# Copies for a triangular inverse issued from ScalarE, the last block's first weights split earlier, and merge steps spaced half a unit apart

## The chip, the cores and the metric

The kernel runs on one core of a Trainium2 chip. A core has five engines with a queue of instructions each: TensorE (PE, matrix products into PSUM), VectorE (DVE), ScalarE (ACT), GpSimd (POOL) and SyncE (SP, which here only issues DMAs). Every engine works its own queue in order; an instruction that waits for another engine holds up everything behind it on its engine. DMAs are issued by an instruction in an engine's queue, and the transfer then runs beside the engines.

The metric is the device time of one execution in microseconds. Before the change three runs took 789.44, 790.56 and 791.85 us; the median, 790.56 us, is the time that the change is measured against.

## What is computed

One decoder layer on a sequence of 256 positions and 2048 channels, in float32. One input projection feeds two token mixers, a gated delta rule (A) and a block attention (B); both are widened, gated, merged, projected and added to the input:

```
h = rms_norm(x, pre_norm_w)
proj = h @ w_in                        # q, k, v, z, b, a of A; q, k, v, z of B; gate_a, gate_b
oa = gated_delta_rule(...)             # chunks of 64; per head and chunk a triangular solve:
#   L = tril(kb @ k.T * decay, -1);  T = inverse(L + I);  u = T @ vb;  w = T @ (kb * exp(g))
u_a = (rms(oa) * silu(z_a)) @ w_branch_a
u_b = (attention(...) * silu(z_b)) @ w_branch_b
merged = sigmoid(gate_a) * u_a + sigmoid(gate_b) * u_b
x = x + rms_norm(merged @ w_out, post_norm_w)
```

## The kernel before

**Products in two parts.** Every float32 weight block is loaded into a raw tile of 1 MB (`raw_...`, a pool with three buffers), and split into a high part that ScalarE makes by a cast (`hi`, L218) and a low part, the difference, that VectorE makes (`lo`, L219). Each pool of split tiles has three buffers. TensorE multiplies high and low parts separately. A raw tile is split in two steps of 128x1024 elements; such a step feeds 16 matmuls in a column block of 256 (`proj_t`), 12 in `proj_n` and in a product for two banks, and 6 in a product for one bank. The loads of weights are issued by SyncE, and each waits there until a raw buffer is free, that is, until the low part of an earlier load (or another reader of it) is done.

**Blocks and background work.** The list `ORDER` (L42) gives the order of the projection blocks: q, k, v, gates and so on. Beside the blocks run generators in queues (`Queue`, L47): after every few matmuls a block calls `tick()`, which counts half a unit of each queue's wait down and, when it has run out, takes the generator's next step. A step emits its instructions at this place of the program; `yield w` asks for `w` units of other work first. So the numbers after `yield` decide where background work stands between the matmuls.

**What keeps order.** An instruction wrapped in `pin()` stays, among the pinned ones of its engine, in the order of the program. All matmuls are pinned. The others (casts and subtractions of `split`, copies from PSUM) are put into the queue of their engine by the framework's scheduler, which works with its own estimate of when inputs are ready; so a change of one instruction can move others.

**The triangles.** For branch A each head writes its triangles to DRAM (`l_d`, from GpSimd, L512). `inverse()` then copies all of them back into `lc`, four times, to 32 partitions each (L635, `LC_WAIT` units apart, pinned on SyncE), and inverts them by 63 pairs of VectorE instructions, `tw<-lc,tv` (L643) and `tv<-tv,tw` (L650). The first of these reads all four copies. At this time TensorE works on the first three blocks of A's values (v0, v1 and v2 in the order; their tiles are named v0, v2 and v4, after the first of a block's two heads), 64 matmuls each: 32 pairs of a `hi` and a `lo` matmul, in four steps of eight pairs. After such a block its results go through `halves` (a ScalarE copy L454, a VectorE addition L455) and `conv_silu` (L461 on VectorE, L462 on ScalarE, three times L464 on VectorE, L468 on ScalarE), for two tiles.

**Seven products.** `seven()` multiplies a 2x2 block matrix by seven products p1 to p7 in place of eight, with sums and differences of the operands; it is used for u_a twice (ua0, ua2, each with four quarters of the gate block ga3 or gb2 as `fill` between the products) and for the first half of the output projection. `fourth()` (L784) forms the operand of p4 in place from the raw weights of p2 (`raw21`) and the third difference, in two halves.

**Merge.** `branch(c)` multiplies branch B's output; `weighted()` (L1062) then multiplies the result by its gate (`gb`, L1065) and adds it to A's part (`ga`, L1068). `merge(c)` (L1112) transposes the sum on TensorE (`mt`) and splits it into `mT` (L1123, L1124), for c = 0 and 1 with the sums that the seven products need (L1126 to L1137). It starts a fixed number of units after `branch(c)` is queued.

**The last block.** The output projection has four column blocks. After the seven products come the second halves of blocks 0 and 1 (four products of 24 matmuls, 5.4 us each); then block 3, whose four loads (quarters of its weights, eight steps) are all split first (six of the steps into tiles named `keep_...`, pinned, L1220 and L1221) so that it can run for the first half of the positions and then for the second. `weigh()` squares and weights each finished bank (L1176, L1177), `finish()` normalizes, adds x and stores.

Of the kernel before, what the change touches and what calls it, by code (L numbers as in the profile page):

```python
# [8 lines left out]
F32 = mybir.dt.float32  # L9
# [3 lines left out]
ALU = mybir.AluOpType  # L13
AX = mybir.AxisListType

P = 128
# [8 lines left out]
D_WAIT = 7  # L25
SC_WAIT = 4
L_WAIT = 5
LC_WAIT = (1.5, 1.5, 1.5, 3.5)
INV = (0.6, 2)
SLOW = 8  # L30
T_WAIT = (5, 7, 7)
# [43 lines left out]
def hybrid_layer(  # L75
# [45 lines left out]
    def acc_tile(name):  # L121
        return acc.tile([P, 512], F32, tag="acc", name=name)
# [493 lines left out]
    def inverse():  # L616
        lc = big.tile([P, 64, 64], F32, tag="u1", name="lc")
        tv = big.tile([P, 16, 64], F32, tag="tv", name="tv")
        tw = big.tile([P, 16, 64], F32, tag="tw", name="tw")

        nc.gpsimd.memset(tv, 1.0)
        for g in range(4):
            nc.gpsimd.affine_select(
                out=tv[32 * g : 32 * g + 32],
                in_=tv[32 * g : 32 * g + 32],
                compare_op=ALU.is_equal,
                fill=0.0,
                base=g,
                pattern=[[4, 16], [-1, 64]],
                channel_multiplier=0,  # L630
            )
        yield 1
        for g in range(4):
            pin(
                nc.sync.dma_start(  # L635
                    lc[32 * g : 32 * g + 32].rearrange("p j i -> p (j i)"), l_d.rearrange("b h j i -> (b h) (j i)")
                )
            )
            yield LC_WAIT[g]
        for j in range(63):  # L640
            n, r = j // 4 + 1, 63 - j
            pin(
                nc.vector.tensor_tensor(  # L643
                    tw[:, :n, :r],
                    lc[:, j : j + 1, j + 1 :].to_broadcast([P, n, r]),
                    tv[:, :n, j : j + 1].to_broadcast([P, n, r]),
                    op=ALU.mult,
                )
            )
            pin(nc.vector.tensor_tensor(tv[:, :n, j + 1 :], tv[:, :n, j + 1 :], tw[:, :n, :r], op=ALU.subtract))  # L650
            yield INV[after[0] > 0]
        for g in range(4):
            nc.gpsimd.dma_start(
                t_d.rearrange("b h (c g) i -> g (b h) c i", g=4)[g], tv[32 * g : 32 * g + 32]
            )
        inv.append(big.tile([P, NT, H, 64], F32, tag="tt", name="tt"))
        for p_ in range(2):
            for t in range(NT):
                nc.gpsimd.dma_start(
                    inv[0][p_ * 64 : p_ * 64 + 64, t, :, :], t_d[2 * t + p_].rearrange("h c i -> c h i")  # L660
                )
        yield L_WAIT
# [30 lines left out]
    def ga(c, t):  # L693
        return ga_[:, c, t, :]
# [48 lines left out]
    def product(a, raw, banks, first, name):  # L743

        for u in range(2):
            hi, lo = split(raw[:, 2 * u : 2 * u + 2, :], [P, 2, 512], f"{name}_{u}")
            for kk in range(2):
                k = 2 * u + kk
                for (ah, al), pt, new in zip(a, banks, first):
                    mm(pt, ah[:, k], hi[:, kk, :], start=(new and k == 0), stop=False, skip_group_check=True)  # L750
                    mm(pt, ah[:, k], lo[:, kk, :], start=False, stop=False, skip_group_check=True)
                    mm(pt, al[:, k], hi[:, kk, :], start=False, stop=(k == 3), skip_group_check=True)
                tick()
# [15 lines left out]
    def seven(quarter, s_, tq, w, c, banks, name, fill=lambda i: None, done=lambda b: None):  # L769
        c11, c12, c21, c22 = banks  # L770
        s5 = tq[0][:, 0]
        product([quarter(0, 0)], load(w, 0, c, name), [c21], [True], f"{name}p1")
        fill(0)
        product([s_[0]], tq[0], [c12], [True], f"{name}p5")
        nc.scalar.copy(c11, c21)
        product([s_[1]], tq[1], [c21], [False], f"{name}p6")
        fill(1)
        nc.scalar.copy(s5, c12)
        raw21 = load(w, 1, c, name)
        nc.vector.tensor_tensor(c12, c21, s5, op=ALU.add)  # L780
        product([quarter(0, 1)], raw21, [c11], [False], f"{name}p2")
        product([s_[2]], tq[2], [c21], [False], f"{name}p7")

        def fourth(u):  # L784
            us = slice(2 * u, 2 * u + 2)
            nc.vector.tensor_tensor(tq[1][:, us], raw21[:, us], tq[1][:, us], op=ALU.subtract)

        fourth(0)
        fill(2)
        nc.vector.tensor_tensor(c22, c21, s5, op=ALU.add)  # L790
        fourth(1)
        done(c11)
        product([s_[3]], load(w, 1, c + 1, name), [c12], [False], f"{name}p3")
        fill(3)
        done(c12)
        done(c22)
        product([quarter(1, 1)], tq[1], [c21], [False], f"{name}p4")
        dq.add(later(lambda: done(c21)))
# [249 lines left out]
    def attention(p):  # L1048
# [7 lines left out]
        for m in range(2):  # L1056
            aq[m].add(attend(h + m, qTs[m], kTs[m]))

    def branch(c):
        pb = proj_n(wb, c * 512, ob_tile(), H, f"ub{c}")  # L1060

        def weighted():  # L1062
            yield 1
            for t in range(NT):
                nc.vector.tensor_tensor(gb_tile()[:, c, t, :], gb_tile()[:, c, t, :], pb[t], op=ALU.mult)  # L1065
            yield 0.5
            for t in range(NT):
                nc.vector.tensor_tensor(ga(c, t), ga(c, t), gb_tile()[:, c, t, :], op=ALU.add)  # L1068

        dq.add(weighted())  # L1070

# [37 lines left out]
    sf = big.tile([P, 4, 4, P], F32, tag="u1", name="sums_f")  # L1109
    summed = []  # L1110

    def merge(c, wait=1):  # L1112
        yield wait
        p3s = []
        for t in range(NT):
            pt = aux_tile(f"mt_{c}_{t}")
            for q in range(4):
                tr(pt[:, q * P : (q + 1) * P], ga(c, t)[:, q * P : (q + 1) * P], ident)
            p3 = pt.rearrange("p (k n) -> p k n", n=P)
            p3s.append(p3)  # L1120
            hi = mT[:, 4 * c : 4 * c + 4, t * P : (t + 1) * P]
            lo = mT[:, 4 * c : 4 * c + 4, S + t * P : S + (t + 1) * P]
            nc.scalar.copy(hi, p3)  # L1123
            nc.vector.tensor_tensor(lo, p3, hi.bitcast(F32), op=ALU.subtract)  # L1124
            if c == 0:
                nc.scalar.copy(sf[:, t], p3)  # L1126
            yield 0.5
        if c == 1:
            nc.vector.tensor_tensor(sf[:, 2], p3s[1], sf[:, 1], op=ALU.add)
            nc.vector.tensor_tensor(sf[:, 3], sf[:, 2], sf[:, 0], op=ALU.subtract)  # L1130
            yield 0.5
            nc.vector.tensor_tensor(sf[:, 1], sf[:, 0], sf[:, 1], op=ALU.subtract)
            nc.vector.tensor_tensor(sf[:, 0], p3s[0], sf[:, 3], op=ALU.subtract)
            for i, j in enumerate((2, 3, 1, 0)):
                yield 1
                nc.scalar.copy(SH[i], sf[:, j])
                nc.vector.tensor_tensor(SL[i], sf[:, j], SH[i].bitcast(F32), op=ALU.subtract)  # L1137
            summed.append(True)
# [7 lines left out]

    for c in range(D // 512):
        branch(c)
        mq.add(merge(c, 2 if c < 3 else 3.5))
        if c == 2:  # L1150
            third(0)

# [44 lines left out]
            (nc.sync if i % 2 == 0 else nc.scalar).dma_start(of[t * P : (t + 1) * P, cs], yw[t][:, cs])  # L1197

    mq.drain()
    for c, banks in ((0, (c11, c21)), (1, (c12, c22))):  # L1200
        for h in range(2, 4):
            product([quarter(0, h), quarter(1, h)], load(wo, h, c, "y"), banks, [False, False], f"y{c}_{h}")
        for t in range(NT):
            weigh(c, t, banks[t])

    c = 3
    pts = [acc_tile(f"a_y{c}_{t}") for t in range(NT)]
    keep = []
    for tg, n in (("g0", 4), ("ga", 4), ("u1", 4)):
        tl = big.tile([P, n, 2, 512], F32R, tag=tg, name=f"keep_{tg}")  # L1210
        keep += [tl[:, i] for i in range(n)]
    parts = []
    for kb in range(KT // 4):
        raw = wraw.tile([P, 4, 512], F32, tag="raw", name=f"raw_y{c}_{kb}")
        nc.sync.dma_start(raw, wo[kb * 512 : (kb + 1) * 512, c * 512 : (c + 1) * 512].rearrange("(k p) c -> p k c", p=P))
        for u in range(2):
            i = kb * 2 + u
            if i < 6:
                hi, lo = keep[2 * i], keep[2 * i + 1]
                pin(nc.scalar.copy(hi, raw[:, 2 * u : 2 * u + 2, :]))  # L1220
                pin(nc.vector.tensor_tensor(lo, raw[:, 2 * u : 2 * u + 2, :], hi.bitcast(F32), op=ALU.subtract))  # L1221
            else:
                hi, lo = split(raw[:, 2 * u : 2 * u + 2, :], [P, 2, 512], f"y{c}_{kb}_{u}")
            parts.append((hi, lo))
            if i in (1, 3):
                weigh(2, i // 2, pts2[i // 2])
    rbs = [so_far(t) for t in range(NT)]
    for t in range(NT):
        for k in range(KT):
# [36 lines left out]
```

## Time and profile before

The profiled execution took 790.14 us, of which 788.4 us are the span from the first to the last instruction; 1.7 us lie around it.

| what | value |
|---|---|
| median of three runs | 790.56 us |
| profiled execution, its span | 790.14 us, 788.4 us |
| VectorE busy, ScalarE busy | 72%, 54% of the span |
| mean DMA rate over the span | 195 GB/s |
| mean granted TensorE clock | 0.993 of full speed |

A row of the timeline or of the chain gives the start in microseconds from the span's start, then the duration, the engine (PEld is TensorE's weight load), the line, the operation, what is written and read, and, in brackets, how long the engine stood idle before it and what ended that. A row of the waits gives who waited for whom: microseconds in total, number of times, and the longest.

### The profile page before, as it was taken

The page shows a single profiled execution, that of the slowest core. Times are in us where ns is not written, and L with a number is a line of the kernel's source. Part 1 is how long each engine was busy: PE and PEld are TensorE (multiplying, and loading weights), DVE is VectorE, ACT ScalarE, POOL GpSimd, SP SyncE. Part 2 cuts the span into 40 slices and gives each one's busy share as a digit, 9 for nine tenths or more (in the row PEclk, how much of TensorE's full clock was granted, in tenths as well). Part 3 has the DMA queues.
Part 4 walks back from the last instruction along what each step waited for, and adds up shares of the span by engine and source line. Part 5 has one row for each costly group of instructions (what it writes and reads, how often), then busy time and mean ns, then how long its engine had stood idle before and what let it go on. Part 6 is the DMA issues. An engine that isn't in the chain of part 4 may idle for free.

```text
span 788.4 us, 10352 instructions
## 1 busy us (share of the span) xinstructions
PE 767.6 (97%) x3923; PEld 652.3 (83%) x3923; DVE 566.0 (72%) x914; ACT 425.1 (54%) x642; POOL 31.5 (4%) x57
## 2 busy tenths in 40 slices
PE   8999999999799999999999999999999999999986
PEld 7898988898588888888888888788887888877864
DVE  5777679886676899775546786775758677877663
ACT  5676665657344444454447574654455544555551
POOL 3000001111000000002001000000000000000000
PEclk9999999999899999999999999999999999999998
DMA  8485666468655657658434557566656855476632
GB/s 307 161 244 202 198 196 170 133 186 220 211 177 197 194 179 204 174 160 241 129 108 165 210 166 257 196 225 225 195 179 214 309 175 200 170 267 215 212 107 107
DMA packets 93656, 153.44 MB, mean 195 GB/s; under 512 B 3237, under 2 KB 46886, under 8 KB 92966
## 3 DMA queue, kind: packets, MB, share of 16 engines
q1 hardware_dynamic: 89094, 136.51, 54.6%
q0 software_dynamic: 3936, 15.21, 5.5%
q10 hardware_dynamic: 576, 1.05, 0.4%
q8 instruction: 31, 0.51, 0.3%
q14 instruction: 19, 0.16, 0.1%
HBM read 149.61 MB, written 3.15 MB: 194 GB/s over the span
## 4 chain that ended last, share of the span: by engine, by line
PE 92%; DVE 4%; ACT 3%; issue 1%; DMA 1%; SPq 0%; DVEq 0%; ACTq 0%
PE a_gb L144 11%; PE a_ga L144 11%; PE a_y L144 10%; PE a_zg L144 6%; PE a_mk L144 6%; PE a_k L144 6%; PE a_v L144 6%; PE a_zm L144 6%; PE a_ub L144 5%; PE a_mq L144 5%; PE a_mv L144 5%; PE a_q L144 4%; PE a_ua L144 4%; PE sv L144 2%; PE s L144 1%
## 5 line engine op out<-in xcount | busy, mean ns | idle before, releaser
L144 PE MATMUL a_ga<-hi_ga,hT 128*128 128x512 f32 x256 | 82.2, 393 | 0.0
L144 PE MATMUL a_gb<-hi_gb,hT 128*128 128x512 f32 x256 | 79.9, 390 | 0.0
L219 DVE TENSOR_TENSOR lo_gb<-raw_gb,hi_gb 128x1024 fp32r<-128x1024 f32 x32 | 38.7, 1223 | 26.1 <-ACT hi_gb L218 26.0
L144 PEld LDWEIGHTS a_gb<-hi_gb,hT 128*128 128x128 f32 x256 | 48.1, 188 | 10.0
L144 PEld LDWEIGHTS a_ga<-hi_ga,hT 128*128 128x128 f32 x256 | 48.1, 188 | 9.8
L219 DVE TENSOR_TENSOR lo_ga<-raw_ga,hi_ga 128x1024 fp32r<-128x1024 f32 x32 | 38.8, 1222 | 19.0 <-ACT hi_ga L218 18.9
L144 PE MATMUL a_v<-hT,hi_v 128*128 128x512 f32 x128 | 47.2, 411 | 5.0 <-ACT hi_v L218 5.0
L144 PE MATMUL a_gb<-lo_gb,hT 128*128 128x512 f32 x128 | 50.4, 394 | 0.5 <-DVE lo_gb L219 0.4
L218 ACT CAST hi_ga<-raw_ga 128x1024 fp32r<-128x1024 f32 x32 | 33.6, 1053 | 31.7 <-PE a_ga L144 18.4
L144 PE MATMUL a_ga<-lo_ga,hT 128*128 128x512 f32 x128 | 50.1, 391 | 0.4 <-DVE lo_ga L219 0.4
L218 ACT CAST hi_gb<-raw_gb 128x1024 fp32r<-128x1024 f32 x32 | 33.4, 1052 | 31.6 <-PE a_gb L144 28.1
L144 PE MATMUL a_zg<-hi_zg,hT 128*128 128x348 f32 (+1 forms) x192 | 47.0, 322 | 0.0
L144 PE MATMUL a_mq<-hT,hi_mq 128*128 128x512 f32 x128 | 46.7, 405 | 0.0
L144 PE MATMUL a_mk<-hT,hi_mk 128*128 128x512 f32 x128 | 46.1, 402 | 0.0
L144 PE MATMUL a_q<-hT,hi_q 128*128 128x512 f32 x128 | 45.7, 397 | 0.0
L144 PE MATMUL a_y<-hi_y,mT 128*128 128x512 f32 x144 | 45.5, 389 | 0.0
L144 PE MATMUL a_ub<-hi_ub,obT 128*128 128x512 f32 x128 | 41.0, 393 | 0.0
L144 PE MATMUL a_zm<-hi_zm,hT 128*128 128x512 f32 x128 | 40.6, 392 | 0.0
L144 PE MATMUL a_k<-hT,hi_k 128*128 128x512 f32 x128 | 40.5, 399 | 0.0
L144 PE MATMUL a_mv<-hi_mv,hT 128*128 128x512 f32 x128 | 40.1, 391 | 0.0
L144 PE MATMUL a_v<-hT,lo_v 128*128 128x256 f32 x128 | 36.9, 288 | 0.5 <-DVE lo_v L219 0.5
L144 PE MATMUL a_q<-hT,lo_q 128*128 128x256 f32 x128 | 35.9, 280 | 0.0
(375 smaller groups left out, 1965.9 us busy)
## 6 DMA issues: line engine op xcount, KB each, us to landing
raw_ga<-in_w_in_dram SPq DMA_DIRECT2D x16, 1024.0 KB, 5.2
raw_gb<-in_w_in_dram SPq DMA_DIRECT2D x16, 1024.0 KB, 5.2
raw_y<-in_w_out_dram SPq DMA_DIRECT2D x15, 1024.0 KB, 5.1
raw_q<-in_w_in_dram SPq DMA_DIRECT2D x8, 1024.0 KB, 5.7
raw_mv<-in_w_in_dram SPq DMA_DIRECT2D x8, 1024.0 KB, 5.1
raw_v<-in_w_in_dram SPq DMA_DIRECT2D x8, 1024.0 KB, 10.7
raw_zm<-in_w_in_dram SPq DMA_DIRECT2D x8, 1024.0 KB, 5.1
raw_mq<-in_w_in_dram SPq DMA_DIRECT2D x8, 1024.0 KB, 5.9
```

The costliest lines, as they stand in the source:

```text
L144: return pin(nc.tensor.matmul(*args, **kwargs))
L218: nc.scalar.copy(hi, raw)
L219: nc.vector.tensor_tensor(lo, raw, hi.bitcast(F32), op=ALU.subtract)
```

## The change

Five edits, the first four of them to where instructions stand, the last to the order of loads and splits at the end:

1. The four copies into `lc` are issued from ScalarE instead of SyncE, with other distances (1.5, 1.5, 1.5, 3.5 units become 2, 2, 2, 2.5, and the first `yield 1` becomes 0.5; the sum stays 9 units).
2. `fourth()` is pinned, so that its two VectorE instructions stand where the program has them: after the splits of p7, and after the split of the third fill.
3. `weighted()` does its four instructions one by one, half a unit apart.
4. `merge(c)` starts when `weighted()` of that c is done, not after a fixed wait.
5. The first two quarters of block 3's weights are loaded and split between the products of blocks 0 and 1 (`last_parts`), and the banks are weighed in another order.

```diff
-LC_WAIT = (1.5, 1.5, 1.5, 3.5)
+LC_WAIT = (2, 2, 2, 2.5)
...
-        yield 1
+        yield 0.5
         for g in range(4):
             pin(
-                nc.sync.dma_start(
+                nc.scalar.dma_start(
                     lc[32 * g : 32 * g + 32].rearrange("p j i -> p (j i)"), l_d.rearrange("b h j i -> (b h) (j i)")
                 )
             )
...
         def fourth(u):
             us = slice(2 * u, 2 * u + 2)
-            nc.vector.tensor_tensor(tq[1][:, us], raw21[:, us], tq[1][:, us], op=ALU.subtract)
+            pin(nc.vector.tensor_tensor(tq[1][:, us], raw21[:, us], tq[1][:, us], op=ALU.subtract))
...
+    merged = []
...
             for t in range(NT):
                 nc.vector.tensor_tensor(gb_tile()[:, c, t, :], gb_tile()[:, c, t, :], pb[t], op=ALU.mult)
-            yield 0.5
+                yield 0.5
             for t in range(NT):
                 nc.vector.tensor_tensor(ga(c, t), ga(c, t), gb_tile()[:, c, t, :], op=ALU.add)
+                yield 0.5
+            merged.append(c)
...
-    def merge(c, wait=1):
-        yield wait
+    def merge(c):
+        while c not in merged:
+            yield 0.5
...
-        mq.add(merge(c, 2 if c < 3 else 3.5))
+        mq.add(merge(c))
...
+    def last_parts(kb):
+        raw = load(wo, kb, 3, "y")
         for u in range(2):
             i = kb * 2 + u
             if i < 6:
...
+    for c, banks in ((0, (c11, c21)), (1, (c12, c22))):
+        for h in range(2, 4):
+            product([quarter(0, h), quarter(1, h)], load(wo, h, c, "y"), banks, [False, False], f"y{c}_{h}")
+            if h == 2:
+                last_parts(c)
+        for t in range(NT):
+            weigh(2 * c, t, (pts2 if c else banks)[t])
+    c = 3
+    pts = [acc_tile(f"a_y{c}_{t}") for t in range(NT)]
+    for kb in range(2, 4):
+        last_parts(kb)
+    for t in range(NT):
+        weigh(1, t, (c12, c22)[t])
```

More of the change, by code (lines that the diff above doesn't have):

```diff
@@ L1199, in hybrid_layer @@
     mq.drain()
[L1200 to L1207, printed above, removed]
     keep = []
@@ L1212, in hybrid_layer @@
     parts = []
-    for kb in range(KT // 4):
-        raw = wraw.tile([P, 4, 512], F32, tag="raw", name=f"raw_y{c}_{kb}")
-        nc.sync.dma_start(raw, wo[kb * 512 : (kb + 1) * 512, c * 512 : (c + 1) * 512].rearrange("(k p) c -> p k c", p=P))
+    def last_parts(kb):
+        raw = load(wo, kb, 3, "y")
         for u in range(2):
@@ L1222, in hybrid_layer @@
             else:
-                hi, lo = split(raw[:, 2 * u : 2 * u + 2, :], [P, 2, 512], f"y{c}_{kb}_{u}")
+                hi, lo = split(raw[:, 2 * u : 2 * u + 2, :], [P, 2, 512], f"y3_{kb}_{u}")
             parts.append((hi, lo))
-            if i in (1, 3):
-                weigh(2, i // 2, pts2[i // 2])
+    for c, banks in ((0, (c11, c21)), (1, (c12, c22))):
[11 more added lines that the diff above has]
+        weigh(1, t, (c12, c22)[t])
     rbs = [so_far(t) for t in range(NT)]
```

## The prediction

> **What bounds the kernel now.** I read the page first: the head line, the busy times, the shares of the chain of waits.
>
> ```profile
> span 788.4 us, 10352 instructions
> PE 767.6 (97%) x3923; PEld 652.3 (83%) x3923; DVE 566.0 (72%) x914; ACT 425.1 (54%) x642; POOL 31.5 (4%) x57
> PE 92%; DVE 4%; ACT 3%; issue 1%; DMA 1%; SPq 0%; DVEq 0%; ACTq 0%
> ```
>
> TensorE is busy 97% of the span and holds 92% of the chain. The change touches no matmul, so it can only remove or add stalls of TensorE (or half clock after one). Next, the waits of PE:
>
> ```profile
> PE a_v L144 <- ACT hi_v L218: 5.0, 1, 5.0
> PE a_y L144 <- ACT keep_g L1220: 1.8, 1, 1.8
> PE a_y L144 <- DVE lo_y L219: 1.2, 2, 0.7
> PE a_y L144 <- DVE keep_g L1221: 0.8, 1, 0.8
> PE a_ga L144 <- DVE lo_ga L219: 0.4, 1, 0.4
> PE a_gb L144 <- DVE lo_gb L219: 0.4, 1, 0.4
> ```
>
> Each edit stands beside one of these: 1 at a_v, 2 at a_ga and a_gb, 2 to 4 at lo_y, 5 at keep_g. Third, I read the timeline around each.
>
> **Edit 1, the values.** Timeline and windows (columns: us, then PE, PEld, DVE, ACT, POOL busy, granted clock, DMA share, GB/s) at the start of the third block, and the chain's row for the matmuls before:
>
> ```profile
> 181.11 19.79 PE a_v L144 x112
> 203.42 0.28 PE L144 MATMUL a_v<-hT,lo_v 128*128 128x256 f32 x1
> 203.74 0.37 ACT L454 COPY y_v<-a_v 128x256 f32<-128x256 f32 x1 [0.98 <-PE a_v L144]
> 204.24 0.42 DVE L455 TENSOR_TENSOR y_v<-a_v,y_v 128x256 f32<-128x256 f32 x1
> 204.69 0.42 DVE L461 TENSOR_TENSOR xp<-y_v,rrow 128x256 f32<-128x256 f32 x1
> 205.69 1.53 DVE L464 SCALAR_TENSOR_TENSOR y_v<-xp,pcol,y_v 128x256 f32<-128x256 f32 x3 [0.58 <-ACT y_v L462]
> 207.25 0.42 ACT L468 ACTIVATE y_v<-y_v 128x256 f32<-128x256 f32 x1 [1.59 <-DVE y_v L464]
> 207.57 2.92 ACT L218 CAST hi_v<-raw_v 128x1024 fp32r<-128x1024 f32 x3
> 208.63 2.36 DVE L219 TENSOR_TENSOR lo_v<-raw_v,hi_v 128x1024 fp32r<-128x1024 f32 x2 [1.02 <-ACT hi_v L218]
> 208.65 0.79 PE L144 MATMUL a_v<-hT,hi_v 128*128 128x512 f32 x1 [4.95 <-ACT hi_v L218]
> 209.91 0.58 PE L144 MATMUL a_v<-hT,lo_v 128*128 128x256 f32 x1 [0.47 <-DVE lo_v L219]
> 214.07 0.40 PE L144 MATMUL a_v<-hT,hi_v 128*128 128x512 f32 x1
> 192.40:203.70 11.30, 11.30 (x65) 9.52 (x63) 7.60 (x15) 4.81 (x9) 0.00 (x0) 1.00 1.01 267
> 203.70:207.10 3.40, 0.00 (x1) 0.00 (x0) 2.68 (x7) 1.30 (x3) 0.00 (x0) 1.00 0.77 281
> 207.10:214.00 6.90, 4.88 (x14) 3.80 (x15) 4.33 (x8) 3.24 (x4) 0.00 (x0) 0.51 0.25 71
> ```
>
> A pair of matmuls takes 19.79/56 = 0.353 us, a block of 32 pairs 11.3; so the blocks end at 192.4 and 203.7. The third should have started at about 203.54 and reached its eighth pair (14 matmuls on, by the x14 of the last window) at 203.54 + 7 x 0.353 = 206.01; it did so at 214.07. Price of the present stall: **8.06 us**, of which 5.11 is the late start (208.65 - 203.54) and 2.95 the lo wait and the half clock (0.51 from 207.1). Cause: on ScalarE the third block's first cast stands behind the whole copy and convolution of the second block. That order is the scheduler's, not the copies'.
>
> In the built program of the change the order on ScalarE is another:
>
> ```
> hi_v0_1_0, hi_v0_1_1, copy 1 into lc, table load, Silu zg x2, copies 2 and 3 into lc,
> y_v0 (L454), y_v1 (L454), hi_v2_0_0, hi_v2_0_1, L462 x2, copy 4 into lc, Silu y_v0, Silu y_v1,
> hi_v2_1_0, hi_v2_1_1, hi_v4_0_0, hi_v4_0_1, y_v2 (L454) ...
> ```
>
> The third block's casts (hi_v4) now stand ahead of the second's convolution: the old stall goes, all 8.06. But the second block's first cast (hi_v2_0_0) stands behind the copy of the first block's second tile, which waits for that block's last matmul. So a stall arises at 192.4, where the window from 192.40 shows none. With the durations above: copy 192.44 to 192.81; cast to 193.86 (2.92 for three, 1.05 as one started alone); first hi matmul at 193.9, 1.4 late. On VectorE the order is L455, L461 twice, then lo: 192.94 + 0.45 + 0.45 = 194.2 after the L455 of 0.42, and lo takes 1.22 (2.36 for two) to 195.4; the second matmul starts at 195.48 where 192.47 + 0.12 was due: 2.9. Then six L464 of 0.51 (1.53 for three) and two Silu of 0.42 stand before hi_v2_1_0: lo 194.2 to 195.4, two steps of lo and six L464 until 199.6, Silu to 200.0, cast to 201.05, lo to 202.3, against a due time of 195.4 + 16.5 x 0.353 = 201.2: 1.1 more. New stalls 2.9 + 1.1 = 4.0; **net -4.1** (8.06 at best; nothing if the new wait grows to the price of the old). I take the value by these rows, since each duration is measured 11 us later on the same instructions.
>
> The clock: in the trace TensorE stood still from 203.70, and the half clock shows from 207.1, 3.4 us on. The new idle pieces are 1.4 and 1.5 us with a matmul between, so I keep full clock. [...]
>
> The four issues move onto ScalarE. Issue cost and landing:
>
> ```profile
> L635 SPq DMA_DIRECT2D lc<-l_d x4: 338/424/462, 184.1 to 185.5; - x4
> DMA to landing us min/median/max: 7.1/10.1/13.2
> DMA to landing us min/median/max: 5.6/10.7/15.7
> L1197 ACTq DMA_DIRECT2D out_dram<-yw x4: 338/338/374, 773.8 to 784.9; - x4
> ```
>
> (second row: tile lc; third: raw_v). An issue from ScalarE takes 0.34 us; copies 1 to 3 fall where the order above has it waiting for TensorE anyway, the fourth where VectorE is the later: 0 (at most 4 x 0.34 = 1.4). On SyncE the weight loads pass the copies; they wait there for raw buffers, not for the copies: 0. Copy 4 is issued only at about 195.9, and VectorE has the first tw, which needs it, ahead of every lo of the third block, due with the 4.0 above at 203.7 + 4.0 - 1.4 = 206.3. So it may take 10.4 us to land. It lands beside one load, not beside three copies and a load: I take the least of its row, 7.1, so 203.0. Cost 0; at 15.7 it would be 5.3 late.
>
> [...]
>
> **Edit 2, u_a.** The pinned subtraction (L786, 1.22) before the second fill:
>
> ```profile
> 505.68 1.22 DVE L786 TENSOR_TENSOR tq_z<-raw_ua,tq_z 128x1024 f32<-128x1024 f32 x1
> 506.82 2.35 DVE L219 TENSOR_TENSOR lo_ga<-raw_ga,hi_ga 128x1024 fp32r<-128x1024 f32 x2
> 507.33 0.39 PE L144 MATMUL a_ga<-hi_ga,hT 128*128 128x512 f32 x1
> 508.09 0.50 PE L144 MATMUL a_ga<-lo_ga,hT 128*128 128x512 f32 x1 [0.37 <-DVE lo_ga L219]
> 514.75 2.58 DVE L219 TENSOR_TENSOR lo_ua0p<-tq_g,hi_ua0p 128x1024 fp32r<-128x1024 f32 x2 [1.49 <-ACT hi_ua0p L218]
> DMA to landing us min/median/max: 5.0/5.2/6.6
> ```
>
> The lo matmul is at 508.09 instead of 507.33 + 0.23 (a step in these stretches): -0.53, twice (a_ga, a_gb). Pinned, the same 1.22 stand in front of the third fill's lo after 517.3: about +0.4 of stall there, and the next gate load, which by the built order waits for the buffer that the third fill's lo frees, issues at 517.33 + 0.6 + 2.35 = 520.3 instead of 517.3 (0.6 is the addition between); by the last row (tile raw_gb, 5.2 median) it lands at 525.5, just late: +0.4; with 6.6 it is 1.4 more. Net +0.25 each: **+0.5** (-1.1 if the cover holds; +0.5 + 2 x 1.4 = +3.3).
>
> **Edits 2 to 4, merge and y.**
>
> ```profile
> 676.47 0.69 DVE L1132 TENSOR_TENSOR sums_f<-sums_f 128x512 f32<-128x512 f32 x1
> 698.12 0.39 PE L144 MATMUL a_y<-hi_y,mT 128*128 128x512 f32 x1
> 699.24 0.50 PE L144 MATMUL a_y<-lo_y,mT 128*128 128x512 f32 x1 [0.73 <-DVE lo_y L219]
> ```
>
> Here lo waits behind the gate additions (the wait row: 1.2 over two places). Spaced out, and with merge tied to them, both go: -1.2. In return the built order puts 11 such additions (0.69, 0.6 from start to start) between two splits of branch B: 11 x 0.6 + 1.2 = 7.8 us, where the splits of a product of 24 matmuls have 24 x 0.23 = 5.5 and their buffers hold a step or two more; I take 0.5 of the 2.3 as late, an estimate (0 to 1.6). And L786 stands before one more lo of y, as at u_a: +0.4. **Net -0.3** (-1.2 to +1.0).
>
> **Edit 5, the last block.**
>
> ```profile
> 755.06 0.39 PE L144 MATMUL a_y<-hi_y,mT 128*128 128x512 f32 x1
> 757.22 0.50 PE L144 MATMUL a_y<-keep_g,mT 128*128 128x512 f32 x1 [1.77 <-ACT keep_g L1220]
> 758.48 2.81 PE L144 MATMUL a_y<-keep_g,mT 128*128 128x512 f32 x11 [0.76 <-DVE keep_g L1221]
> ```
>
> With half of the weights split before, TensorE goes on at its step of 0.23: (757.22 - 755.06 - 0.23) + (758.48 - 757.22 - 0.23) = 1.93 + 1.03 = **-2.96**. The moved splits (casts of 1.0, subtractions of 1.2) lie beside products of 5.4 us that have two splits each; with two more VectorE has 4 x 1.2 = 4.8. Without that cover the gain would be 0.
>
> **Sum** against the profiled 790.14: -4.1 + 0.5 - 0.3 - 3.0 = -6.9, so 783.2; the profiled run lies 0.42 under the median 790.56, so **783.6** on the median.
>
> **The rivals.**
> - *The new wait also halves the clock.* For: the old one did. Against: pieces of 1.5 us. It would add the 2.95 of the old wait, less the 1.1 that the second stall then absorbs: +1.9, 785.5.
> - *The wait only moves.* One of the largest waits goes from the third block to the second at its whole price, since a copy still waits for a block's end; copies 2 and 3 are built together, so "in turn" isn't what runs. Edit 1 gains nothing: 783.6 + 4.1 = 787.7. For: the order above. Against: only the copy, not the convolution, precedes the cast.
> - *All gains are eaten:* edit 1 at 0, edit 5 half, and u_a at its bound: 783.6 + 4.1 + 1.5 + 2.8 = 792.0 at worst, about 790.5 with half of that load's lateness.
> - *Slower: copy 4 lands late.* The first tw holds VectorE's queue, every lo of the third block behind it, and TensorE waits. It decides from 10.4 us of landing; at 13.2 it costs 2.8, at 15.7 5.3 and, being over 3.4 us of idleness, the 2.95 of half clock: 791.9; at 17 us 793.2. For: the row of raw_v has 15.7 behind four copies. Against: one load beside it.
>
> **How the numbers follow.** Forecast 780 to 785: 0.55; clock 0.12; wait moves 0.17; gains eaten 0.08; slower 0.08. What can be told from no change is 0.3%, 2.4 us. Of the moved wait 0.11 counts as faster and 0.06, where u_a's bound adds to it, as the same; gains eaten as the same. Faster 0.55 + 0.12 + 0.11 = 0.78, same 0.14, slower 0.08. The range goes from 780.0 (edit 1 with half of its new stalls, 783.6 - 2.0, and u_a without its cost, -1.6) to 789.5, which leaves out late copies and eaten gains; the forecast's own is 780 to 785.
>
> **What would show it.** Right: no wait of keep_g; a_y without the 1.2; the third block at full clock; at 192.4 a wait of a_v for hi_v of 1.4 and for lo_v of 1.5 with the clock at 1.00, another of about 1 at 201. Wrong: a clock near 0.5 after 195; the first tw ending after 206 with lo_v behind it; a wait of a_ga for the raw tile's DMA over 1 us; a new wait in block 0 or 1 of y.

## The result and the profile after

The changed kernel took 782.22 us, the median of four executions (782.20 to 782.77), against 790.59 (four executions): a ratio of 0.9896, 95% interval 0.9878 to 0.9913. A second set of four on another chip gave 783.64 (782.76 to 784.46) against 790.48, 0.9911 (0.9895 to 0.9927). So the change saves 6.8 to 8.4 us; the prediction was 783.6.

Page and waits of the changed kernel, as shown of before:

```profile
span 780.4 us, 10345 instructions
PE 765.1 (98%) x3923; PEld 651.2 (83%) x3923; DVE 564.1 (72%) x914; ACT 424.7 (54%) x642; POOL 31.5 (4%) x57
...
PE a_v L144 <- DVE lo_v L219: 1.4, 2, 0.8
PE a_v L144 <- ACT hi_v L218: 1.4, 1, 1.4
PE a_ga L144 <- DVE lo_ga L219: 0.7, 2, 0.4
PE a_gb L144 <- DVE lo_gb L219: 0.4, 1, 0.4
PE a_y L144 <- DVE lo_y L219: 0.4, 1, 0.4
```

The 5.0 of a_v for hi_v has become 1.4, in another place; both waits for keep_g are gone; lo_y has one wait in place of two, lo_ga two in place of one.

Since the 3923 matmuls are the same, each can be compared with its twin. TensorE's place against before (negative: earlier), read from the starts of the same matmul in both traces, gives a ledger of the span:

```
place in the program                  after - before   step of it     forecast
first block of values begins              +0.10           +0.10          0
values done                               -4.25           -4.35         -4.1
before ua0                                -4.35           -0.10          0
after ua0                                 -3.88           +0.47         +0.25
after ua2                                 -3.57           +0.31         +0.25
branch B done                             -3.11           +0.46   }
seven products of y, blocks 0 and 1       -4.39           -1.28   }     -0.3
block 3 done                              -8.03           -3.64         -3.0
```

The last row is the whole difference of the spans, 788.43 - 780.40. The +0.46 at branch B is not a wait: four transposes of a merge stand behind the last matmul of branch B before (it starts at 694.71) and ahead of it in the changed kernel (691.60). The first row is of before, the second of the changed kernel:

```profile
694.94 0.60 PE L147 MATMUL mt<-ident,ga 128*128 128x128 f32 x4
690.00 0.60 PE L147 MATMUL mt<-ident,ga 128*128 128x128 f32 x4
```

So TensorE does this work earlier, and the next row gets the 0.46 back: without it, branch B is at 0 and y at -0.82.

**Values.** TensorE, ScalarE and VectorE from the start of the second block to that of the third, then two windows of 3.41 us with the granted clock:

```profile
192.54 0.37 ACT L454 COPY y_v<-a_v 128x256 f32<-128x256 f32 x1 [2.46 <-PE a_v L144]
192.81 1.99 ACT L218 CAST hi_v<-raw_v 128x1024 fp32r<-128x1024 f32 x2
193.91 0.51 PE L144 MATMUL a_v<-hT,hi_v 128*128 128x512 f32 x1 [1.41 <-ACT hi_v L218]
193.95 1.22 DVE L219 TENSOR_TENSOR lo_v<-raw_v,hi_v 128x1024 fp32r<-128x1024 f32 x1
194.08 0.31 ACTq L635 DMA_DIRECT2D lc<-l_d  x1
195.23 0.38 PE L144 MATMUL a_v<-hT,lo_v 128*128 128x256 f32 x1 [0.81 <-DVE lo_v L219]
201.67 0.39 PE L144 MATMUL a_v<-hT,lo_v 128*128 128x256 f32 x1 [0.63 <-DVE lo_v L219]
202.19 1.05 ACT L218 CAST hi_v<-raw_v 128x1024 fp32r<-128x1024 f32 x1 [0.88 <-DMA raw_v<-in_w_in_dram]
202.67 0.22 DVE L643 TENSOR_TENSOR tw<-lc,tv 128x63 f32<-128x63 f32 x1
203.27 1.23 DVE L219 TENSOR_TENSOR lo_v<-raw_v,hi_v 128x1024 fp32r<-128x1024 f32 x1 [0.38 <-ACT hi_v L218]
205.40 0.36 ACT L454 COPY y_v<-a_v 128x256 f32<-128x256 f32 x1
207.19 0.40 PE L144 MATMUL a_v<-hT,hi_v 128*128 128x512 f32 x1
207.43 0.28 PE L144 MATMUL a_v<-hT,lo_v 128*128 128x256 f32 x1
...
190.19:193.60 3.41, 2.31 (x14) 1.75 (x12) 1.01 (x3) 1.06 (x2) 0.00 (x0) 1.00 1.02 218
193.60:197.01 3.41, 2.29 (x11) 1.80 (x12) 3.34 (x6) 2.01 (x4) 0.00 (x0) 1.00 0.89 217
```

The three new waits stand where they were forecast. The rows list 1.41, 0.81 and 0.63 us of idle time; by the starts of the twin matmuls they make TensorE 1.57, 1.19 and 0.89 us later, against 1.4, 1.5 and 1.1 forecast. The second is shorter because lo began at 193.95, not 194.2: the two L461 took 0.75 together, not 0.9. Behind the third, TensorE is 3.56 us late in all (forecast 4.0). The clock stayed at 1.00. The third block's first cast, at 202.19, now stands ahead of the copy of the second block's results, at 205.40, and the block starts at 207.19 without a wait. Copy 4 landed 7.97 us after its issue, at 202.05, in time for the first tw at 202.67, whose row shows no idle time. That is 0.62 us for VectorE. For TensorE the margin is larger: the matmul at 207.43 reads the lo of 203.27, which takes 1.23, so by these rows copy 4 could have come some 3 us later (an estimate).

**u_a.** PE, ScalarE and SyncE at the third and the last fill of ua0:

```profile
503.21 0.39 PE L144 MATMUL a_ga<-lo_ga,hT 128*128 128x512 f32 x1
512.22 1.22 DVE L786 TENSOR_TENSOR tq_z<-raw_ua,tq_z 128x1024 f32<-128x1024 f32 x1
514.62 0.50 PE L144 MATMUL a_ga<-lo_ga,hT 128*128 128x512 f32 x1 [0.37 <-DVE lo_ga L219]
515.73 0.37 SPq L766 DMA_DIRECT2D raw_ga<-in_w_in_dram  x1
521.04 2.00 ACT L218 CAST hi_ga<-raw_ga 128x1024 fp32r<-128x1024 f32 x2 [2.52 <-DMA raw_ga<-in_w_in_dram]
523.40 0.50 PE L144 MATMUL a_ga<-lo_ga,hT 128*128 128x512 f32 x1 [0.31 <-DVE lo_ga L219]
```

The matmul at 503.21 has lost its wait. The one at 514.62 has it instead, behind the pinned subtraction. And the last gate load, issued at 515.73 (forecast 520.3 - 4.4), lands 5.3 us later; the cast waits for it and the matmul at 523.40 is late, as the prediction has it.

**The end.** The row that stood at 755.06 and the start of block 3:

```profile
750.66 0.39 PE L144 MATMUL a_y<-hi_y,mT 128*128 128x512 f32 x1
750.89 2.43 PE L144 MATMUL a_y<-keep_g,mT 128*128 128x512 f32 x10
```

From 750.66 to 750.89 it is 0.23, the usual step: no wait.

### The profile page after: what moved, and what is told of

The parts are those of the page before. It is cut to its first block, busy times and chain, and to the rows that moved or that the text cites. A ratio compares the mean times of both kernels' runs of the same rounds, so it can differ in the third digit from the quotient of the medians.

```text
span 780.4 us, 10345 instructions
## 1 busy us (share of the span) xinstructions
PE 765.1 (98%) x3923; PEld 651.2 (83%) x3923; DVE 564.1 (72%) x914; ACT 424.7 (54%) x642; POOL 31.5 (4%) x57
## 4 chain that ended last, share of the span: by engine, by line
PE 91%; DVE 3%; ACT 3%; DMA 2%; issue 1%; SPq 0%; DVEq 0%; ACTq 0%
PE a_gb L144 11%; PE a_ga L144 11%; PE a_y L144 10%; PE a_zg L144 6%; PE a_mk L144 6%; PE a_k L144 6%; PE a_ub L144 6%; PE a_zm L144 6%; PE a_mq L144 5%; PE a_mv L144 5%; PE a_v L144 5%; PE a_q L144 4%; PE a_ua L144 3%; PE sv L144 2%; PE s L144 1%
## 5 line engine op out<-in xcount | busy, mean ns | idle before, releaser
L144 PE MATMUL a_v<-hT,hi_v 128*128 128x512 f32 x128 | 45.4, 398 | 1.4 <-ACT hi_v L218 1.4
## 6 DMA issues: line engine op xcount, KB each, us to landing
raw_v<-in_w_in_dram SPq DMA_DIRECT2D x8, 1024.0 KB, 10.7
```

Of the source, the lines that this page charges most:

```text
L144: return pin(nc.tensor.matmul(*args, **kwargs))
```

## The experiments

Each ran beside the kernel before on the same chip; a ratio is against those runs. "Place" is TensorE's place against before, as in the ledger.

**e1_alone: edit 1 alone on the kernel before.**

```diff
-LC_WAIT = (1.5, 1.5, 1.5, 3.5)
+LC_WAIT = (2, 2, 2, 2.5)
...
-        yield 1
+        yield 0.5
...
-                nc.sync.dma_start(
+                nc.scalar.dma_start(
```

> The kernel before with edit 1 alone (the four copies issued from ScalarE, with the new distances). In the built program the order of ScalarE around the value blocks is that of the changed kernel, and the rest is that of before. If the gain of edit 1 is the order of the casts: TensorE is 4.3 us earlier after the value blocks than before, and stays so, the clock stays at 1.00 there, and the span is 788.4 - 4.3 = 784.1 (time about 786.2). If the gain needs the other edits, or most of it came from them: under 2 us.

Ten executions from 785.04 to 789.08, median 787.92, ratio 0.9966 (0.9952 to 0.9980). In the profile the place goes from +1.23 to -2.41: 3.64 gained at the values. The waits there are those of the changed kernel (1.41 and 0.81). But the record of the clock shows a half-speed stretch of 3.41 us from 196.3 (granted 0.53 from 196.08 to 199.49, 0.97 in the next 3.41), and one after the wait for keep_g from 756.1, which costs another 1.03 there. The mechanism holds; the size is cut by a clock that the changed kernel's own profile did not show, and the spread of 4 us is unusual. That became a question of its own (changed_again).

**e1_undone: the changed kernel with the copies back on SyncE.**

```diff
-                nc.scalar.dma_start(
+                nc.sync.dma_start(
```

> The changed kernel with the four copies issued from SyncE again, with the new distances kept. Built, the third block's casts stand behind the second block's convolution again, as before. If the order is what counts: the 4.95 us wait of a_v for hi_v and the half clock come back, and the span is 780.4 + 4.3 = 784.7 (time about 786.6). If it is the distances (copies further apart, less crowding of the weight load): the wait stays away and the time stays at 782.

787.35, ratio 0.9961 (0.9946 to 0.9976). The old wait is back:

```profile
PE a_v L144 <- ACT hi_v L218: 4.9, 1, 4.9
```

and with it 6.83 us at half clock from 208.4. The place goes from +0.57 to +0.91 over the values: nothing gained. So the distances alone do nothing; with them, the move to ScalarE's queue is what flips the scheduler's order. The move with the old distances was not run.

**order_alone, order_on_sync, order_on_scalar: the order written out.** The splits of the second and third block are pinned, the copies of a block's results stand behind the next block's second cast and the convolution behind the fourth:

```diff
-                hi, lo = split(raw[:, :, m * P : (m + 1) * P], [P, 8, P], f"{name}_{kb}_{m}")
+                if held is None:
+                    hi, lo = split(raw[:, :, m * P : (m + 1) * P], [P, 8, P], f"{name}_{kb}_{m}")
+                else:
...
+                    pin(nc.scalar.copy(hi, raw[:, :, m * P : (m + 1) * P]))
+                    pin(nc.vector.tensor_tensor(lo, raw[:, :, m * P : (m + 1) * P], hi.bitcast(F32), op=ALU.subtract))
+                    if m == 1 and held:
+                        held.pop(0)()
...
-        vTs = [halves(pv_[m], f"v{h + m}") for m in range(2)]
-        for m in range(2):
-            conv_silu(vTs[m], 2 * H + h + m)
-            vq.add(v_tok(h + m, vTs[m]))
...
+        if p < 2:
+            v_held.extend((first, second))
```

(`first` holds the copies, `second` the convolution; for the third and fourth block both run at once, as before.)

On the kernel before, with nothing of the change:

> The kernel before with nothing of the change, but the order of the value blocks written out as in order_on_sync (copies into lc on SyncE at the old distances). If the gain of edit 1 is the order that the scheduler chose, and neither the queue nor the distances: TensorE is 6.3 us earlier than before after the value blocks (as there: from +1.08 to -5.27), more than edit 1's 4.3; the rest is as before: span 788.4 - 6.3 = 782.1 at the same start, up to 1.2 more at a later one, and 1 to 2 us more where the clock falls at the last block's wait for keep_g (time 783.8 to 787). If the order pays only together with the other edits: less than 4.

784.50 (783.44 to 785.01), ratio 0.9911 (0.9893 to 0.9929). The place goes from +0.44 to -6.34: 6.8 gained with the copies on SyncE at their old distances, where edit 1 gained 4.35.

On the changed kernel with the copies on SyncE:

> The changed kernel with the copies issued from SyncE, and the order of the casts written out instead: the splits of the second and third block are pinned, the copies of a block's results come behind the next block's second cast, and its convolution behind the fourth. If the order alone makes the gain, and the queue of the copies none, both stalls go: none at 192.4; at the third block the load's landing (202.6 before, for a cast due at 203.5) is what is left, cast to 203.6 and lo to 204.9 where 203.7 is due, some 1.2 us. So 6.8 us earlier than before after the value blocks against 4.3 of the change: span 780.4 - 2.5 = 777.9 (time about 779.7). If the copies on SyncE themselves do harm (loads behind them): not faster than 782.

780.65 (780.15 to 781.48), ratio 0.9878 (0.9863 to 0.9893); the place goes from +1.08 to -5.27, 6.35 gained. What is left at the values is one wait:

```profile
PE a_v L144 <- DVE lo_v L348: 0.8, 1, 0.8
```

with 0.2 for hi_v ahead of it; the cast itself waits 3.82 us for the third block's load, which lands at 203.9.

And with the copies on ScalarE:

> As order_on_sync, with the copies issued from ScalarE as in the change: this and that kernel differ in the queue of the copies alone. If the queue is worth nothing by itself: after the value blocks within 0.5 us of order_on_sync's gain of 6.35, where the load for the third block lands (202.1 in the changed kernel, 202.6 before) sets what is left of the wait; time within 0.6 us of 780.65. If ScalarE's issue helps or hurts: a difference of over 1 us in the same stretch.

780.03 (778.83 to 783.19), ratio 0.9864 (0.9832 to 0.9896); from +0.51 to -6.70, 7.2 gained. That is 0.85 more than on SyncE there, but 0.4 more than order_alone, also on SyncE: beyond the expected 0.5 in one comparison and inside it in the other. The kernel best, further down, has the same value blocks as order_on_sync and gains 6.82 there (from +0.41 to -6.41), so one arrangement differs by 0.5 between two executions. The times overlap. So the queue is worth less than a microsecond by itself, if anything, and the order 6 to 7.

**moved_wait: the convolution ahead of the second block's casts.**

```diff
-        if p < 2:
+        if p == 1:
             v_held.extend((first, second))
```

(on the kernel of order_on_scalar)

> The changed kernel with the first block's copies and its whole convolution ahead of the second block's first cast (pinned), the third block's casts ahead as in the change. This is the rival in which the wait only moves, made on purpose. By the rows of before: the cast starts after copy, two L455, two L461, six L464 and a Silu, at about 197.5, so the first matmul is 6 us late; being over one stretch of 3.41 us idle, the clock halves for 6.83 us as it did at 207, 3 us more: 9 in place of the 3.8 that the change pays there, so span 780.4 + 5.2 = 785.6 (time about 787.4). If the place in the program matters beyond the order: another sum by 2 us or more.

789.08 (786.80 to 790.22), ratio 0.9968 (0.9956 to 0.9979). Waits and windows:

```profile
PE a_v L144 <- ACT hi_v L347: 5.7, 1, 5.7
...
190.75:194.16 3.41, 3.41 (x21) 2.95 (x21) 0.43 (x1) 0.37 (x1) 0.00 (x0) 1.00 1.00 203
194.16:197.58 3.42, 0.82 (x5) 0.45 (x4) 1.92 (x6) 1.28 (x3) 0.00 (x0) 1.00 0.84 181
197.58:204.41 6.83, 3.29 (x9) 2.50 (x10) 5.13 (x8) 3.64 (x5) 0.00 (x0) 0.50 0.88 218
```

The place goes from +2.56 to +2.37: of the 4.35 that the change gains there 0.2 is left. So the moved wait costs 7.9, not 9 (5.7 idle, not 6, and less lost at half clock), and the span comes to 787.2 with a start 2.5 us late. The rival of the moved wait would have been real, had the scheduler put the convolution there too.

**e5_alone: edit 5 alone on the kernel before** (its part of the diff as shown).

> The kernel before with edit 5 alone. If the splits beside the products are free and the last block's waits are the whole effect: both waits of keep_g go (1.93 and 1.03) and with them the small later ones, 0.6 by the traces of before and after: span 788.4 - 3.6 = 784.8 (time about 786.9). If part of the 3.6 came from the other edits' order: 3.0 or less.

786.06 (785.40 to 787.59), ratio 0.9943 (0.9926 to 0.9959). The place goes from +1.06 to -2.55: 3.61, as expected. Edit 5 stands by itself.

**pin_alone and pin_undone: edit 2.**

```diff
-            nc.vector.tensor_tensor(tq[1][:, us], raw21[:, us], tq[1][:, us], op=ALU.subtract)
+            pin(nc.vector.tensor_tensor(tq[1][:, us], raw21[:, us], tq[1][:, us], op=ALU.subtract))
```

On the kernel before:

> The kernel before with edit 2 alone. If the ledger is right: 0.8 us later than before after ua2 (0.47 + 0.33), the waits of a_ga and a_gb for lo at two places each instead of one, and in y 0.5 less for the wait of 711.86 and 0.4 more for the one near 723: span 788.4 + 0.7 = 789.1 at the same start (time about 791.2). By the prediction's own terms (0.25 each): 0.5 to 0.9.

792.55 (791.65 to 794.21), ratio 1.0024 (1.0014 to 1.0033): slower. The place goes by +0.39 at ua0, +0.60 at ua2 and -0.14 in y, 0.85 together where 0.7 was expected. The -0.14 is the wait of 711.86 gone (-0.78) and one near 723 come (+0.64). In this execution 3.41 us at half clock after the wait for keep_g add 1.1 more, which the expectation didn't have.

Taken from the changed kernel:

> The changed kernel with fourth() free of the pin. By the two profiles, the pin cost 0.47 us at ua0 and 0.33 at ua2; in y the built order without it puts the subtraction between the two splits of p6, where a late lo would cost up to 0.7, and takes the 0.37 wait of 718.3 away. If the ledger is right: TensorE is 0.8 us earlier after ua2 than in the changed kernel, and the span is 780.4 - 0.8 = 779.6 (time about 781.4), 779.2 if y gains its 0.4 too. If the pin is what holds something else together: not faster than 782.2.

781.96 (781.78 to 782.72), ratio 0.9892 (0.9875 to 0.9910). Against the changed kernel -0.46 at ua0 and -0.32 at ua2, as expected; in y the free subtraction makes lo of p6 late (+0.79) and the wait of 718.3 goes (-0.69): +0.10 there. 0.7 us better by the trace; the times overlap.

**merge_alone: edits 3 and 4 on the kernel before** (their parts of the diff as shown).

> The kernel before with edits 3 and 4 alone. If they are what takes the waits of a_y for lo_y: the wait of 699.24 goes (0.9), the one of 711.86, which stands behind the free subtraction, stays or halves (0 to -0.7), and branch B is 0.46 later at its last block: span 788.4 - 0.45 to 788.4 - 1.1 (time 789.4 to 790.1). If they only move the work: no change in TensorE's place at the start of y's third product beside branch B's 0.46.

Ten executions, four from 788.72 to 790.30 and six from 792.19 to 792.74, median 792.25; ratio 1.0011 (0.9997 to 1.0025). In the profiled one (790.11) the place goes by +0.47 at branch B and by -1.19 in y. The 0.47 are the four transposes again, so the net is -0.72: the wait of 699.24 gone (-0.73), the one of 711.86 moved to p6 (-0.78 and +0.77). The six others have a mean granted clock of 0.990 to 0.991 against 0.993.

**changed_again: the changed kernel once more.**

> The changed kernel once more, for the spread of its executions. In the single look at edit 1 alone the clock fell to half for 3.41 us after the same 1.4 + 0.8 us of idleness at 192 to 196 that left it at 1.00 in the changed kernel's profile; there a fixed grid of 3.41 us stretches put 2.15 us of the idleness in one stretch, here 1.10 and 1.12 in two. If the grid's place decides: most executions near 782.2 at a mean clock of 0.998, and about one in four or five some 1 to 1.7 us slower at a clock near 0.996. If the drop belongs to the other kernel: none.

In the profiled execution the clock fell:

```profile
192.66:196.08 3.42, 1.46 (x7) 0.77 (x5) 2.02 (x4) 2.43 (x4) 0.00 (x0) 1.00 0.93 200
196.08:199.49 3.41, 3.15 (x10) 2.77 (x11) 3.34 (x7) 0.93 (x3) 0.00 (x0) 0.50 1.28 326
```

Here the same waits leave 1.46 us of work in one stretch; in the first profile 2.31 and 2.29 in two. The half clock costs 1.42 us up to the third step (from +1.12 to +2.54 against the first profile), and the wait that stood there takes 0.89 of it back: 0.53 net. At the end of the third block 0.22 of it is left, since a pair of matmuls takes 0.347 us there against 0.353 in the first profile; why is open. The four executions spread over 1.7 us, without the clear two groups that I expected; a part of that is the start, 1.1 us later in this profile at the first value block.

**best: order_on_sync with the pin of fourth() taken away.**

> order_on_sync with fourth() free of the pin: the changed kernel's edits 3 to 5, the new distances on SyncE, the order of the value blocks written out. If the terms add: 0.7 us less than order_on_sync (779.7), span 779.0 at its start, 778.0 at an early one (time 779.6 to 780.7), and faster than both kernels.

779.57 (779.46 to 780.51), ratio 0.9853 (0.9836 to 0.9870), its interval below the changed kernel's 0.9878 to 0.9913. Span 777.55, a place of -10.9 at the end. Its waits in the value blocks and later:

```profile
PE a_v L144 <- DVE lo_v L348: 0.8, 1, 0.8
...
PE a_y L144 <- DVE lo_yp L219: 0.5, 1, 0.5
PE a_ga L144 <- DVE lo_ga L219: 0.4, 1, 0.4
PE a_gb L144 <- DVE lo_gb L219: 0.4, 1, 0.4
```

## Why the prediction came out, step by step

- **Edit 1, -4.1: measured -4.35, by the forecast's mechanism.** The old wait went with its half clock, a new one came at the second block. e1_undone and order_alone show that neither queue nor distances carry the gain, only the order on ScalarE. The new waits were put at 4.0 and measured 3.56. That would be a gain of 4.50; the ledger shows 0.15 less because, behind its stall, the kernel before took 0.347 us for a pair in the third block and the changed kernel 0.353. **The clock's term, 0, was luck.** That pieces of 1.4 and 1.5 us leave the clock alone was my estimate, which no row of before shows: the same waits halved the clock in changed_again (0.50 from 196.08 to 199.49) and in e1_alone (0.53 there). In the first profile the idle time lay in two stretches of 3.41 us, 1.10 and 1.12 us, and the clock stayed at 1.00.
- **The issues on ScalarE: free, but for another reason in part.** Copies 2 and 3 were expected behind the Silu of zg; they were issued before it (last section). Copy 4 came at 194.08, not 195.9, and took 8.0 us instead of 7.1, two errors that partly cancel: it landed at 202.05, where 203.0 was forecast. The late copy didn't happen in any profile; how late it may land wasn't tried.
- **Edit 2 in u_a, +0.5: +0.78.** Both mechanisms were right (the subtraction ahead of the third fill, the gate load late). The costs were 0.55 and 0.60 at ua0 instead of 0.4 each. pin_alone shows that the pin by itself is a loss.
- **Edits 2 to 4 in y and branch B, -0.3: -0.82.** This term was right in sign and wrong in its parts. The 0.5 for late splits at branch B did not come: the 0.46 of the ledger are the four transposes, which y gives back, and that it looks like the 0.5 is chance. The two waits for lo_y gave 1.51 by twin matmuls (0.73 at 699.24, 0.78 at 711.86), where I took the 1.2 of idle time in the row of waits; the new wait costs 0.69, not 0.4. And the cause of the second wait was misread. Only the lo of 699.24 stands behind gate additions; that of 711.86 stands behind the subtraction of fourth(), in the kernel before:

```profile
709.45 1.22 DVE L786 TENSOR_TENSOR tq<-raw_y,tq 128x1024 f32<-128x1024 f32 x1
710.59 2.35 DVE L219 TENSOR_TENSOR lo_y<-raw_y,hi_y 128x1024 fp32r<-128x1024 f32 x2
```

  So edits 3 and 4 take the first wait (merge_alone), and the second goes with the pin (pin_alone), which puts the new one in its place.
- **Edit 5, -2.96: -3.64.** The two waits gave 3.09; the other 0.55 are three small waits at later steps of the block, of 0.1 to 0.2 each, which no row of waits lists and which comparing the matmuls one by one shows. e5_alone has the same 3.61.
- **Sum:** -6.9 forecast, -8.0 in the spans, -6.8 and -8.4 in the medians. The terms missed by 0.25, 0.28, 0.5 and 0.7, three of the four on the pessimistic side.
- **The rivals.** "The clock halves too" was given 0.12 at 1.9 us: it does occur, in some executions. It cost 0.53 us net in changed_again (0.22 by the end of the third block) and 0.7 in e1_alone, so in size it is a part of the forecast's spread. But the reason given against it, pieces of 1.5 us, did not hold. "The wait moves" needed the convolution ahead of the cast (moved_wait). Eaten gains and the late copy did not show.

## What to carry to other kernels

Where a scheduler places the instructions that are not pinned, moving one instruction to another queue can win by the order that it happens to cause; read the built order, find the work that matters (here: the next block's cast ahead of the last block's post-processing), and write that order down. It brought 6 to 7 us here in place of 4.35. Price a wait by the place of the matmuls behind it, twin against twin, not by the idle time that is listed. And look at the clock behind short waits close together: waits of 1.41 and 0.81 us left it at 1.00 in the changed kernel's profile and were followed by 3.41 us at 0.50 in changed_again, at 0.53 us net.

## What the runs showed of the hardware

**The same waits left the clock alone in one profile and halved it in another.** In the profile of the kernel before the granted clock fell at 207.14, rose at 213.96 and fell again at 783.99 us: 6.83 and 570.03 us apart, 2 and 167 times 3.413. Two kernels with the same wait for keep_g, in windows of 3.41 us:

```profile
748.09:751.50 3.41, 1.47 (x6) 0.65 (x4) 2.07 (x3) 3.03 (x6) 0.00 (x0) 1.00 0.00 0
751.50:754.91 3.41, 2.83 (x7) 2.25 (x8) 3.41 (x5) 3.41 (x8) 0.00 (x0) 0.50 0.16 16
```

in order_alone, and in merge_alone

```profile
753.95:757.37 3.42, 1.65 (x7) 0.94 (x5) 1.73 (x3) 2.69 (x6) 0.00 (x0) 1.00 0.00 0
757.37:760.78 3.41, 2.65 (x12) 2.06 (x12) 3.41 (x4) 3.41 (x7) 0.00 (x0) 1.00 0.01 3
```

In order_alone 1.47 us of work in a window and the next one is at 0.50; in merge_alone 1.65 us and the next one is at 1.00. In the value blocks it was 1.46 us in changed_again, with 0.50 behind it, and 2.31 and 2.29 us in the changed kernel's profile, with 1.00. The ends of matmuls are modelled, so the second decimal is soft. The prediction saw one fall, 3.4 us after TensorE stopped, and took pieces of 1.4 and 1.5 us for safe; in changed_again the longest wait in the window was 1.41 us. What decides beyond these rows is open.

Whether a half-clock stretch behind the wait for keep_g that edit 5 removes (2.5 us of idleness in 3.0) is a part of what parts the executions of merge_alone into two groups is not shown either. The six with the longer time have the lower mean clock, but only one execution has a trace, such a stretch cost 1.1 us in pin_alone while the groups lie 1.9 us apart or more, and the kernel before, run beside them, went from 788.98 to 792.45 with a mean clock of 0.991 to 0.993.

**DMA issues went out before the work ahead of them on their engine was done.** ScalarE's queue holds copy 1, table load, two Silu, copies 2 and 3 in this order. The timeline of the changed kernel:

```profile
183.94 1.05 ACT L218 CAST hi_v<-raw_v 128x1024 fp32r<-128x1024 f32 x1 [1.59 <-PE a_v L144]
184.28 0.83 ACTq L635 DMA_DIRECT2D lc<-l_d  x2
185.01 1.28 ACT L585 ACT_TABLE_LOAD   x1
185.14 0.45 ACTq L635 DMA_DIRECT2D lc<-l_d  x1
186.30 0.99 ACT L585 ACTIVATE zg<-a_zg,rstd 128x348 f32<-128x348 f32 x2
```

Copy 1 goes out inside the cast ahead of it, copies 2 and 3 before the two Silu ahead of them have begun. Copy 4, at 194.08, lies inside the casts of 192.81 to 194.80, 0.04 us after the second L461 ended (193.29 + 0.75), for which the L462 ahead of it wait. What holds an issue back is not shown: this is read from these rows, and no run tests it.

**The weight load behind the copies was slow on either queue.** Landing of raw_v and lc in the changed kernel (least, median, most):

```profile
DMA to landing us min/median/max: 5.7/10.7/15.8
DMA to landing us min/median/max: 6.9/8.4/11.1
```

15.8 us for the third block's first load with three copies issued by ScalarE before it; 15.7 before, with four by SyncE, where the median of raw_v is 10.7 in both. So the move bought an order, not a faster load.
